# Max pooling of a 128 MiB input on one core: which run of memory each partition takes

## The chip, the cores and the metric

The kernel runs on one core of a Trainium2 chip. The metric is device time in microseconds for one launch. In three runs the kernel before took 334.78, 335.02 and 334.77 us; the median is 334.78 us.

## What is computed

An input of 32 x 256 x 4096 numbers (float32, 134.2 MB) is pooled along its last axis to 256 outputs: each output is the maximum of one window of 4096 / 256 = 16 neighbouring numbers.

```python
for i in range(output_size):                 # output_size = 256
    start = int(i * length / output_size)    # length = 4096
    end = int((i + 1) * length / output_size)
    result[:, :, i] = np.max(x[:, :, start:end], axis=-1)
```

Windows don't overlap, and input and output lie in memory in the same order. So the whole problem is one list of 32 x 256 x 256 = 2,097,152 windows of 16 numbers (64 bytes), each of which gives one number; 134.2 MB are read and 8.39 MB written.

## The kernel before

**Tiling.** The list of windows is shared among the 128 partitions of SBUF, 16,384 windows for each. It is cut into two groups that follow one another in memory. Group A has 9,340 windows for each partition, group B 7,044. Inside a group, the part of memory is cut into 128 unbroken *runs* of equal length: 9,340 x 64 = 597,760 bytes in A, 7,044 x 64 = 450,816 bytes in B. Partition p takes run p. The function `group` (L64) makes the two views for this: `xg` of the input, 128 rows of n x 16 numbers (L70), and `og` of the output, 128 rows of n numbers (L71).

**Loads.** The loop over groups (L77) and over the loads of a group (L80) takes a slice of columns from every run at once. One load brings 1,024 windows to each of the 128 partitions, 65,536 bytes for each and 8.39 MB in all. Group A is walked from its end to its start: a first small load of 128 windows (L87), eight of 1,024, and one of 1,020. Group B is walked forward: six of 1,024, and a last one of 900. That makes 17 loads, all issued from the queue of SP (SyncE) at L87 and L96.

**Buffers.** `ring` (L48) holds two buffers for each partition, each 152 windows (`GAP`) longer than a chunk of 1,024. Loads take the two in turn. Each time that a buffer comes round, the load is put at the other end of it, so that it overlaps the previous content by 872 windows only.

**Reductions.** VectorE makes each load into maxima with `reduce_max` (`pooled`, L54 to L60; L56 in the profile): one instruction for 872 windows, whose place the next load into this buffer needs, and then one for the other 152. The results go to `kept` (L49), which holds the output of all but the last load. A load that reuses a buffer waits for the long reduction of the load two before it. The last load of 900 windows is reduced in one instruction into a free end of `ring` (`last_kept`).

**Stores.** The two large stores, one for each group, are issued on SP at L117, behind all loads on the same queue: 4,670 KB for A and 3,072 KB for B. The last 900 results of each partition go out from the queue of ACT (ScalarE) at L114, 450 KB. Stores use `og`, so they take the same way back as the loads.

## Time and profile before

| what | value |
|---|---|
| median of three runs | 334.78 us |
| span of the profiled execution, from first to last instruction | 333.1 us |
| read from memory, written to memory | 134.22 MB, 8.39 MB |
| `reduce_max` of 872 windows | 14,686 ns, 14 of them |
| `reduce_max` of 152 windows | 2,676 ns, 15 of them |
| `reduce_max` of the last 900 windows | 15,143 ns |
| VectorE's waits for loads | 51.5 us in total |
| issue to landing: first load, a full load (median), last load | 4.7, 24.0, 21.7 us |
| issue to landing: the stores of A and B, the last store | 32.4 and 18.2, 4.2 us |

The profiled execution's span is 1.7 us shorter than the median of the runs. Busy shares are taken over the whole span. "Issue to landing" runs from the instruction on the queue to the last of its bytes, and holds the time in which a DMA stands behind earlier ones. A "packet" in the profile is one piece that one of the 16 DMA engines moves. A chain of waits names, for each stretch of time, what the work that ended last was held up by.

### The profile page before, as it was taken

The numbers are of one execution on the slowest core, as the hardware profiler recorded it, in microseconds if no ns is written. First come the engines' busy times: TensorE is split into PE (matmuls) and PEld (weight loads), VectorE is DVE, ScalarE is ACT, GpSimd is POOL, SyncE is SP. The second block draws the span as 40 slices with busy tenths as digits, with TensorE's granted clock in tenths as the row PEclk, the third lists the DMA queues.
The fourth block names the chain that finished last, engine by engine and source line by source line (L and its number), as shares of the span: only waits on it lengthen the run. The fifth ranks groups of instructions, "written<-read, shape, count | busy, mean of one in ns | idle before, by whom it ended". The sixth has DMA issues, their size and how long they took to land.

```text
span 333.1 us, 113 instructions
## 1 busy us (share of the span) xinstructions
DVE 276.5 (83%) x32; POOL 0.2 (0%) x4
## 2 busy tenths in 40 slices
DVE  2009979797997979799797979979797998979993
POOL 0000000000000000000000000000000000000000
DMA  9898989899898989899898989899898989899997
GB/s 378 378 504 378 504 378 504 378 449 433 378 504 378 504 378 504 378 441 441 384 494 377 504 378 504 378 456 425 386 496 378 504 378 504 378 458 443 393 395 330
DMA packets 2880, 142.61 MB, mean 428 GB/s; under 512 B 320, under 2 KB 320, under 8 KB 448
## 3 DMA queue, kind: packets, MB, share of 16 engines
q1 hardware_dynamic: 2736, 142.15, 98.8%
q10 hardware_dynamic: 144, 0.46, 0.3%
HBM read 134.22 MB, written 8.39 MB: 428 GB/s over the span
## 4 chain that ended last, share of the span: by engine, by line
DMA 57%; DVE 36%; DVEq 5%; issue 0%; SPq 0%
DMA ring<-in_x_dram 57%; DVE kept L56 36%; DVEq L148 5%; SPq L87 0%
## 5 line engine op out<-in xcount | busy, mean ns | idle before, releaser
L56 DVE TENSOR_REDUCE kept<-ring 128x152 f32<-128x2432 f32 (+3 forms) x31 | 261.4, 8473 | 51.5 <-DMA ring<-in_x_dram 51.5
L56 DVE TENSOR_REDUCE ring<-ring 128x900 f32<-128x14400 f32 x1 | 15.1, 15143 | 0.0
L134 POOL MEMSET const-bfloat16-1.0<- 128x1 bf16 x1 | 0.1, 103 | 0.0
L134 POOL MEMSET const-uint8-127<- 128x1 uint8 x1 | 0.1, 102 | 0.0
L134 POOL MEMSET const-float32-0.0<- 128x1 f32 x1 | 0.1, 100 | 0.2 <-issue 0.2
L134 POOL MEMSET const-float32-1.0<- 128x1 f32 x1 | 0.1, 99 | 0.0
## 6 DMA issues: line engine op xcount, KB each, us to landing
ring<-in_x_dram SPq DMA_DIRECT2D x1, 8160.0 KB, 23.9
ring<-in_x_dram SPq DMA_DIRECT2D x1, 7200.0 KB, 21.7
out_dram<-kept SPq DMA_DIRECT2D x1, 4670.0 KB, 32.4
out_dram<-kept SPq DMA_DIRECT2D x1, 3072.0 KB, 18.2
ring<-in_x_dram SPq DMA_DIRECT2D x1, 1024.0 KB, 4.7
out_dram<-ring ACTq DMA_DIRECT2D x1, 450.0 KB, 4.2
ring<-in_x_dram SPq DMA_DIRECT2D x14, 24.0
```

The source lines that it names most:

```text
L56: nc.vector.reduce_max(out=dst, in_=ring[:, at * W : (at + n) * W].rearrange("p (n w) -> p n w", w=W), axis=mybir.AxisListType.X,)
L134: nc = _bacc.Bacc("TRN2", target_bir_lowering=False, num_devices=1)
L148: with _tile.TileContext(nc) as tc:
```

## The change

In a group, partition p = 8 i + j (i from 0 to 15, j from 0 to 7) takes run 16 j + i in place of run p. The view of memory that had 128 rows now has two levels, 16 (i) by 8 (j): a step of i is one run, a step of j is 16 runs. The tile in SBUF keeps its 128 partitions; the numbers of both sides are paired in order, so that i x 8 + j counts the partitions. The output uses the same assignment, so that every result goes to its own place. The function `by_run` gives back the tile's rows as they are.

```diff
+    RUNS = 16
...
+    def by_run(tile_rows):
+
+        return tile_rows
+
...
         return (
-            xw[span].rearrange("(p n) w -> p (n w)", p=P),
-            ow[span].rearrange("(p n) -> p n", p=P),
+            xw[span].rearrange("(j i n) w -> i j (n w)", i=RUNS, n=n),
+            ow[span].rearrange("(j i n) -> i j n", i=RUNS, n=n),
         )
...
-            xn = xg[:, a * W : (a + n) * W]
+            xn = xg[:, :, a * W : (a + n) * W]
...
-                    out=ring[:, CHUNK * W : (CHUNK + n) * W], in_=xn
+                    out=by_run(ring[:, CHUNK * W : (CHUNK + n) * W]), in_=xn
...
-                nc.sync.dma_start(out=ring[:, at * W : (at + n) * W], in_=xn)
+                nc.sync.dma_start(
+                    out=by_run(ring[:, at * W : (at + n) * W]), in_=xn
+                )
...
-        stores.append((og[:, 0:full], kept[:, base : base + full]))
+        stores.append((og[:, :, 0:full], by_run(kept[:, base : base + full])))
...
-    nc.scalar.dma_start(out=og[:, full : full + last], in_=last_kept)
+    nc.scalar.dma_start(out=og[:, :, full : full + last], in_=by_run(last_kept))
```

The partition of a run changes, and with it the order in which a DMA names the runs of memory. The sizes of the groups and loads, the buffers, the reductions, the queues and the order of issue are as before.

## The prediction

> **What bounds the kernel now.** I read the page from its top down, to see which engine has no time left.

> ```profile
> span 333.1 us, 113 instructions
> ...
> DVE 276.5 (83%) x32; POOL 0.2 (0%) x4
> ...
> DMA packets 2880, 142.61 MB, mean 428 GB/s; under 512 B 320, under 2 KB 320, under 8 KB 448
> ...
> q1 hardware_dynamic: 2736, 142.15, 98.8%
> q10 hardware_dynamic: 144, 0.46, 0.3%
> ```

> The two queues keep the 16 DMA engines busy for 98.8 + 0.3 = 99.1% of 333.1 us, which is 330.1 us of packet time; only 3.0 us of the span is left idle. VectorE has 17% to spare. The median of the runs, 334.78 us, is 1.7 us above the profiled span; I add these 1.7 us to every span that I work out.

> Next the chain of waits, because its shares can mislead: it gives DMA 57% and VectorE 36%, as if VectorE were half of the bound.

> ```profile
> 39.49 23.96 DMA ring<-in_x_dram
> 63.45 0.02 issue
> 63.48 14.70 DVE kept L56
> 78.17 0.02 issue
> 78.19 23.97 DMA ring<-in_x_dram
> ```

> A load is issued when the long reduction (14.70 us) has freed its buffer, and lands 23.96 us later. Issue to issue along the chain is 38.70 us, and two loads land in it, so one load takes 19.35 us. The issue stands 23.96 - 19.35 = 4.61 us before the previous load has landed: the queue never runs dry, and the reductions on the chain only set when an issue may go. The timeline says the same from VectorE's side: 17.28 us of work for each load, then 2.07 to 2.08 us of waiting for the next.

> ```profile
> 63.48 17.28 DVE L56 TENSOR_REDUCE kept<-ring 128x872 f32<-128x13952 f32 x2 [2.07 <-DMA ring<-in_x_dram]
> 82.83 17.28 DVE L56 TENSOR_REDUCE kept<-ring 128x872 f32<-128x13952 f32 x2 [2.08 <-DMA ring<-in_x_dram]
> ```

> Last, the rate in single stretches: one of loads, one after the last load, in which nearly only the two stores of `kept` move.

> ```profile
> 24.80:44.10 19.30, 17.26 (x2) 0.00 (x0) 1.00 1.00 435
> 313.00:328.00 15.00, 14.96 (x1) 0.00 (x0) 1.00 1.01 436
> ```

> The last two columns are the DMA share and GB/s. Loads read memory and write SBUF, stores do the opposite, and both stop at the same 435 GB/s, 27.2 for each of 16 engines. A limit of memory would hardly be the same for reads and writes, so I place the limit on the DMA engines or on their way to SBUF. So there is nothing to gain at memory, and everything to lose at SBUF.

> How an engine gets its work follows from one more window, that of one load.

> ```profile
> DMA packets 144, 8.39 MB, mean 419 GB/s; under 512 B 16, under 2 KB 16, under 8 KB 16
> ```

> 128 packets of data, one for each partition (65,536 bytes), and 16 small ones, one for each engine: an engine moves 8 partitions, one after the other. Check: 8 x 65,536 bytes at 27.2 GB/s is 19.3 us.

> **The change, part by part.**

> *Instructions.* 17 loads, 3 stores and 32 reductions stay, on the same queues in the same order; no wait is added. An issue on SP takes about 0.33 us now (the row for `in_x_dram` has 327/328/426 ns). A three-level pattern may take longer; between 0 and twice that is 0 to 0.33 us, times 17 is 5.6 us at most. The 4.61 us by which an issue is early hides it: I take 0. Were that cover gone, 5.6 us would show.

> *VectorE.* Each partition has the same number of windows as before: 0.

> *The rows themselves.* A packet still moves one unbroken piece of one run, 65,536 bytes in a chunk, so packets should stay 2880 and their bytes 142.61 MB: 0.

> *Which runs are read together.* Before, neighbouring partitions read neighbouring runs; now the partitions 8i to 8i + 7 read runs i, 16 + i, ..., 112 + i. Sixteen streams of 65,536-byte pieces remain, a whole run (597,760 or 450,816 bytes) or more apart. A gain is bounded by the idle 3.0 us; a loss here has no row. At a limit that reads and writes share I take 0, with the 3.0 us as lower end.

> *Which engine gets which partitions.* This is the large term. Before, both sides of a DMA count 128 on the outside, and any split of 128 rows into 16 lots of 8 will do. Now memory counts 16 x 8 and the tile counts 128. The lot that can be cut off the outer 16 is one i, and its partner on the tile is 8i to 8i + 7: eight neighbouring partitions, taken in order j = 0 to 7. Whether the split before was this one the trace doesn't show, nor does it show two engines at one part of SBUF. So the bounds: below, 0 (the split was the same, or neighbourhood is free); above, two engines share a way at all times, and every packet takes twice its time: + 330.1 us. More than two together would cost more, but to that no row gives a bound, and I leave it outside.

> Between ends that far apart I go by the nearest row, the 99.1% of the queues: a way that one engine fills has nothing left for a second, and each two that meet halve. I take the upper end, less what the engines' unequal starts save. The first 6 us, in slices of 0.15 us, show these.

> ```profile
> DMA  0000000000099922598999999999999999000000
> ```

> The engines start in the eleventh to twelfth slice and all are busy by the eighteenth or nineteenth, some 1.1 us; two partners would be about 0.3 us apart (my estimate, a quarter of that). An engine that is ahead by 0.3 us works alone for so long before its partner comes and leaves it alone as long at the end, 0.6 us in each of 19 DMAs on the SP queue, 11 us. The sum: 330.1 x 2 - 11 + 3.0 = 652 us of span, + 1.7 = **654 us**.

> [...]

> *Where the stall goes.* VectorE's 17.28 us a load are covered better than before: it would wait some 21 us a load. At the end, the last reduction (15.14 us) and its store (4.2 us to landing) lie beside the stores of `kept`, 17.8 us now and some 35 us then, so the end stays with the queues.

> **The rivals.**

> *A. The partners drift apart.* Nothing in the profile holds two engines in step, except that none gets its next load before VectorE has freed a buffer. If sharing is uneven, one gets ahead by d (in time at full rate), and a load whose lot changes its way once, in the middle, takes 38.7 - 2d. The lead lasts d x T / 19.35 of a load time T, and can't pass T - 14.70, the time between an issue and the landing before it. Together: T x T = 38.7 x 14.7, T = 23.9 us and d = 7.4 us. 142.61 / 8.39 = 17.0 loads x 23.9 + 3.0 + 1.7 = **411 us** as the far end. For it: the starts differ already; against it: in the trace of before the loads keep equal times to 0.02 us, so nothing seems to push engines apart. Everything from 400 to 600 us belongs here.

> *B. No change, the other side.* The lots are dealt as before by some other way of pairing, or neighbours don't meet: 330.1 + 3.0 + 1.7 = **334.8 us**. It decides as soon as a load takes 19.35 us. For it: both directions run at the same 27.2 GB/s an engine, so the engine itself may be the limit, and partitions may not matter.

> *C. A little faster.* Runs that lie side by side are opened together, the ramp of the first load gets shorter and the queue idles less: down to 334.8 - 3.0 = **331.8 us**, if all idle time went. It needs B's condition too. Against it: the steady loads are at 435 GB/s and give nothing.

> *D. It doesn't do what it says:* the pattern might fold back into one step of 128. It can't: from j = 7 of one i to j = 0 of the next, memory steps back by 111 runs. But if the split fell to 8 engines, twice the lots on each would give the 663 to 665 us of the upper bound too; the number of small packets would tell it (8 for each DMA, not 16).

> **The numbers.** Forecast (600 to 670 us) 0.58; A (400 to 600) 0.22; a small loss or one over 670 us 0.03; B 0.09; C 0.08. The time is the forecast's, 654 us. The range goes from the lower end of A, 400, to the full doubling, 330.1 x 2 + 3.0 + 1.7 = 665, and a little over, 670; it holds 0.80. Slower has 0.58 + 0.22 + 0.03 = 0.83, same 0.09, faster 0.08, where 0.2% (0.7 us) is about what a measurement of this kernel can tell from no change.

> **What would show it.** Landings 38 us apart in place of 19.35; issue to landing 2 x 38 - 14.7 = 61 us in place of 24.0; about 215 GB/s in the stretch of loads and in that of stores alike; still 144 packets a load and 2880 in all, at a DMA share still near 99% because waiting packets count as busy; VectorE's 276.5 us of work unchanged, its waits up from 51.5 to some 370 us. I am wrong if a load still takes 19.35 us, or if loads slow down and stores don't, for then memory and not SBUF is where engines meet.

## The result, and the profile after

The changed kernel takes **683.58 us** (median of 6 runs, 682.07 to 685.85) beside 335.04 us for the kernel before (334.77 to 335.36, 6 runs): 2.0407 times as long, 95% interval 2.0381 to 2.0433. The forecast was slower, 654 us; the range ended at 670 us, 14 us short. The span of the profiled execution is 680.3 us, against 652 in the working.

From the page of the changed kernel, the lines that answer to the first ones of the prediction:

```profile
span 680.3 us, 113 instructions
...
DVE 276.6 (41%) x32; POOL 0.2 (0%) x4
...
DMA packets 2880, 142.61 MB, mean 210 GB/s; under 512 B 320, under 2 KB 320, under 8 KB 448
...
q1 hardware_dynamic: 2736, 142.15, 99.2%
q10 hardware_dynamic: 144, 0.46, 0.2%
...
another core or an unknown queue 50%; DVE 40%; DMA 7%; SPq 0%; issue 0%; DVEq 0%
```

The same instructions, packets and bytes, and still full queues: 99.2 + 0.2 = 99.4% of 680.3 us is 676.2 us of packet time, 2.05 times the 330.1 us before. A queue that is "busy" says nothing about its speed; bytes over time do (210 GB/s against 428). The chain of waits no longer names most of the loads; it says "another core" on a kernel with one core, and why it does isn't shown. The view of all waits still names them:

```profile
DVE kept L57 <- DMA ring<-in_x_dram: 369.6, 16, 38.1
DVE ring L57 <- DMA ring<-in_x_dram: 18.2, 1, 18.2
```

VectorE waits 387.8 us for loads (the second line is the wait for the last one), where it waited 51.5. The timeline of the changed kernel gives the price of one load, and two stretches of it the rate of loads (above) and of the stores after the last landing (below):

```profile
88.71 17.28 DVE L57 TENSOR_REDUCE kept<-ring 128x872 f32<-128x13952 f32 x2 [23.12 <-DMA ring<-in_x_dram]
129.12 17.28 DVE L57 TENSOR_REDUCE kept<-ring 128x872 f32<-128x13952 f32 x2 [23.12 <-DMA ring<-in_x_dram]
```

```profile
120.00:160.00 40.00, 17.28 (x2) 0.00 (x0) 1.00 1.01 210
649.00:664.00 15.00, 14.80 (x1) 0.00 (x0) 1.00 1.00 281
```

One load takes 129.12 - 88.71 = 40.41 us, not 38.70, which is twice the 19.35 before. The stores run at 281 GB/s: slowed too, but less. Issue to landing of a full load is 66.1 us, which is 2 x 40.4 - 14.7, as the ring wants it.

The single packets of 65,536 bytes in the trace's records tell the most. Before, each takes 2.42 us. The records name no engine, but where one packet ends and the next begins an engine's packets can be joined. After the change, eight of one engine's packets in a row, from 127.2 us on, read in ns:

```
4905 5107 5121 5109 | 4915 5107 5109 5119
```

Two fours, each with a first packet 0.2 us shorter: something changes after four packets, which by the prediction's lots is after four partitions. Inside a four a packet takes 5.11 us, 2.11 times as long as before.

### The profile page after: what moved, and what is told of

It is laid out like the page before. It is cut to its first block, busy times and chain, and to the rows that moved or that the text cites. A ratio compares the mean times of both kernels' runs of the same rounds, so it can differ in the third digit from the quotient of the medians.

```text
span 680.3 us, 113 instructions
## 1 busy us (share of the span) xinstructions
DVE 276.6 (41%) x32; POOL 0.2 (0%) x4
## 2 busy tenths in 40 slices
DMA packets 2880, 142.61 MB, mean 210 GB/s; under 512 B 320, under 2 KB 320, under 8 KB 448
## 3 DMA queue, kind: packets, MB, share of 16 engines
q1 hardware_dynamic: 2736, 142.15, 99.2%
HBM read 134.22 MB, written 8.39 MB: 210 GB/s over the span
## 4 chain that ended last, share of the span: by engine, by line
another core or an unknown queue 50%; DVE 40%; DMA 7%; SPq 0%; issue 0%; DVEq 0%
DVE kept L57 38%; DMA ring<-in_x_dram 7%; DVE ring L57 2%; SPq L92 0%; DVEq L57 0%
## 5 line engine op out<-in xcount | busy, mean ns | idle before, releaser
L57 DVE TENSOR_REDUCE kept<-ring 128x152 f32<-128x2432 f32 (+3 forms) x31 | 261.4, 8472 | 369.6 <-DMA ring<-in_x_dram 369.6
## 6 DMA issues: line engine op xcount, KB each, us to landing
ring<-in_x_dram SPq DMA_DIRECT2D x14, 66.1
```

Of the source, the lines that this page charges most:

```text
L57: nc.vector.reduce_max(out=dst, in_=ring[:, at * W : (at + n) * W].rearrange("p (n w) -> p n w", w=W), axis=mybir.AxisListType.X,)
```

## The experiments

**Which part is it: the lots of partitions, or the order of the runs?** Two kernels, called e1 and e2 from here on, each change one without the other. The first, e1, keeps the lots of eight partitions and gives the runs their old places:

```diff
-        span = slice(taken * P, (taken + n) * P)
+        span = slice(taken, taken + RUNS * (8 * n + 1))
...
-            xw[span].rearrange("(j i n) w -> i j (n w)", i=RUNS, n=n),
+            xw[span].rearrange("(i q) w -> i (q w)", i=RUNS)[
+                :, 0 : 8 * n * W
+            ].rearrange("i (j f) -> i j f", j=8),
```

> Partition p takes run p again, as before the change, but memory still counts 16 x 8 on the outside: the 16 blocks of eight runs stand one window apart, so that the two levels can't become one. The last load has 899 windows, and some 100 of the 2,097,152 windows are left out. Theory 'lots' (an engine that gets eight neighbouring partitions shares its way to SBUF with another): a load takes 40.4 us as after the change, the median is 680 to 685 us. Rival 'order' (runs 16j + i read together are slow for memory): a load takes 19.35 us, 335 us.

Measured: 689.02 us. The timeline of this kernel:

```profile
89.07 17.28 DVE L57 TENSOR_REDUCE kept<-ring 128x872 f32<-128x13952 f32 x2 [23.21 <-DMA ring<-in_x_dram]
129.58 17.28 DVE L57 TENSOR_REDUCE kept<-ring 128x872 f32<-128x13952 f32 x2 [23.23 <-DMA ring<-in_x_dram]
```

40.51 us a load, with every run where it was before the change. The order of the runs is not needed for the loss. The total is 4 us above the forecast of "lots", because 36 us passed from the last landing to the end, in place of 31. The stores are hardly slower: in the first 15 us after the last landing the stores move 276 GB/s (281 in the changed kernel), but the second large one waits here for the store of the last results and is issued at 669.7 us only (at 631.1 us in the changed kernel).

The second kernel, e2, keeps two levels and neighbouring runs read together, and lets the lots be dealt otherwise:

```diff
-    RUNS = 16
+    RUNS = 32
```

> The change with 32 x 4 in place of 16 x 8: partition 4i + j takes run 32j + i. Neighbouring runs are still read together and memory still has two levels, but an outer count of 32 lets each engine have two separate fours of partitions. Theory 'lots': 19.35 us a load, within 0.5% of before, 333.5 to 336 us. Rivals 'order' and 'pattern' (any two-level pattern is slow): 600 us and over.

Measured over 11 runs: 335.59 us, 1.0017 times before (1.0008 to 1.0026). Its timeline, and the same two lines of the kernel before:

```profile
0.72 0.67 SPq L92 DMA_DIRECT2D ring<-in_x_dram  x1
...
5.89 2.29 DVE L57 TENSOR_REDUCE kept<-ring 128x128 f32<-128x2048 f32 x1 [5.89 <-DMA ring<-in_x_dram]
...
44.59 17.28 DVE L57 TENSOR_REDUCE kept<-ring 128x872 f32<-128x13952 f32 x2 [2.08 <-DMA ring<-in_x_dram]
```

```profile
0.73 0.38 SPq L87 DMA_DIRECT2D ring<-in_x_dram  x1
...
5.44 2.29 DVE L56 TENSOR_REDUCE kept<-ring 128x128 f32<-128x2048 f32 x1 [5.44 <-DMA ring<-in_x_dram]
```

Neither the order of the runs nor a two-level pattern costs the kernel its speed. What is left, 0.56 us, is mostly in these lines: the first issue takes 0.67 us in place of 0.38, and the first load lands 0.45 us later. No earlier load covers the first one, a case that the prediction's "4.61 us of cover" passed over. That an outer count of 32 gives an engine two separate fours is how e2 was meant; which partitions an engine gets stands in no record.

**How many engines, how many ways?** A *way* is the prediction's word for the path to a part of SBUF that two engines may have to share; no record shows one, only the times of packets. The kernel e3 has an outer count of 8:

```diff
-    RUNS = 16
+    RUNS = 8
```

> The change with 8 x 16: partition 16i + j takes run 8j + i. Eight engines carry data, 8 small packets a DMA, 136 packets in all for a load. Theory 'lots': engines e and e + 2 now stand 32 partitions apart and share, so four ways are in use at a time: 4 x 2 x 10.1 = 80.8 us a load, some 1375 us. If engines didn't meet but only their number counted: 38.7 us a load, 665 us.

Measured: 1277.87 us. From its page and its timeline:

```profile
DMA packets 2720, 142.61 MB, mean 112 GB/s; under 512 B 160, under 2 KB 160, under 8 KB 288
...
q1 hardware_dynamic: 2584, 142.15, 49.7%
```

```profile
172.37 17.28 DVE L57 TENSOR_REDUCE kept<-ring 128x872 f32<-128x13952 f32 x2 [62.68 <-DMA ring<-in_x_dram]
252.29 17.28 DVE L57 TENSOR_REDUCE kept<-ring 128x872 f32<-128x13952 f32 x2 [62.64 <-DMA ring<-in_x_dram]
...
1098.53 17.28 DVE L57 TENSOR_REDUCE kept<-ring 128x872 f32<-128x13952 f32 x2 [56.62 <-DMA ring<-in_x_dram]
1171.71 17.28 DVE L57 TENSOR_REDUCE kept<-ring 128x872 f32<-128x13952 f32 x2 [55.91 <-DMA ring<-in_x_dram]
```

2720 = 20 x 136, with 8 small packets a DMA (160 in 20): eight engines, half of the queues' time (49.7%). A load takes 79.9 us at first, as engines that share have it (80.8), and not 38.7; the expected total was 8% too high, since a load shrinks to 73.2 us by the end. Here partners seem to drift apart: one packet in four is shorter than the rest, by the records 4.6 to 5.0 us near 90 us and 3.0 to 3.7 us near 1,041 us.

**Loads and stores apart.** In one kernel (e7) the loads alone have the new pattern, in the other (e8) the stores alone.

> Loads as after the change, stores as before it (the output is in another order). With the stores alone 15.6 us were lost; if the two parts only add up, this is the change less 15.6 us: 668 us, with 40.4 us a load, and the stores of 7.74 MB take 18 us from the last landing on.

> Loads as before the change, stores as after it (the results of a partition go to the run that the change would have loaded, so the output is in another order). If stores double as loads did: 8.19 MB, 18.8 us more and some 0.4 us for the longer issue, 354 us. If their engines part with time, as after the change, where the end after the last landing took 30 us in place of 20: 345 to 348 us. If only loads collide: 335.5 us.

Measured: loads alone 671.99 us; stores alone 350.55 us, 1.0462 times before (1.0445 to 1.0479). The two losses, 337.2 us (beside 334.82 for the kernel before) and 15.6 us (beside 334.98), come to 4 us more than the whole change lost. The stretch after the last landing, in the kernel with changed stores alone:

```profile
313.00:345.00 32.00, 15.19 (x2) 0.00 (x0) 1.00 0.98 236
```

Stores read SBUF, and they are slowed as well: 236 GB/s against the 436 before. Neither of the first two forecasts for the stores was hit: the loss lies between 10 to 13 and 19 us.

**Twelve small loads, the partitions alone different.** This (e9) measures the disputed price by itself, ahead of the kernel before:

```diff
+    nc.sync.dma_start(out=ring[0:65:64, 0 : 2048 * W], in_=rows(2))
+    nc.sync.dma_start(out=ring[0:5:4, 0 : 2048 * W], in_=rows(2))
+    nc.sync.dma_start(out=ring[0:2:1, 0 : 2048 * W], in_=rows(2))
+    nc.sync.dma_start(out=ring[0:33:32, 0 : 2048 * W], in_=rows(2))
...
+    nc.sync.dma_start(out=ring[0:4:1, 0 : 2048 * W], in_=rows(4))
...
+    nc.sync.dma_start(out=ring[0:16:1, 0 : 2048 * W], in_=rows(16))
```

> The kernel before, and ahead of it twelve small loads one after the other, each with one row of 128 KB (two packets of 65,536 bytes) for each engine that takes part; the rows' bytes are not used. Only the partitions differ. An engine alone: 2 x 2.42 us, and 2.2 us around it (the first small load: 4.7 us to landing for 8 packets of 0.31), 7.0 us to landing. Theory 'ways' (the partitions of one four, and of the four 32 further up, are written through one way of 27.2 GB/s): partitions 0 and 64, 0 and 4, or eight partitions 4 apart: 7.0 us. 0 and 1, or 0 and 32, or 16 partitions 8 apart, or 16 partitions 4 apart: two engines to a way, 2 x 5.1 + 2.2 = 12.4 us. 0 to 3, or 0 to 15: four to a way, 22.5 us. If a pair alone shows 4.84 us for a packet and only sixteen engines 5.1 us, the 4.4% over the doubling come with the number of engines that wait; if a pair shows 5.1 us, they are the price of two engines on one way. Partitions 0, 32, 64, or 0 to 64 in steps of 16: an engine without a partner keeps 2.42 us a packet if pairs are independent, and is slower if those that wait hold up the others. If engines only compete for memory, all loads of two rows take 7.0 us.

Each load writes where the one before wrote, so SP's queue waits for the landing at the next line: L59 waits for the load of L58 (partitions 0 and 64), L60 for 0 and 4, L61 for 0 and 1, L62 for 0 and 32, L65 for 0 to 3, L67 for eight partitions 4 apart, L69 for sixteen 4 apart, L104 for 0 to 15. From the queue's waits, longest first:

```profile
SPq L104 <- DMA ring<-in_x_dram: 20.8, 1, 20.8
SPq L65 <- DMA ring<-in_x_dram: 20.6, 1, 20.6
...
SPq L69 <- DMA ring<-in_x_dram: 12.1, 1, 12.1
...
SPq L61 <- DMA ring<-in_x_dram: 11.4, 1, 11.4
...
SPq L62 <- DMA ring<-in_x_dram: 10.9, 1, 10.9
...
SPq L60 <- DMA ring<-in_x_dram: 7.1, 1, 7.1
SPq L59 <- DMA ring<-in_x_dram: 6.8, 1, 6.8
SPq L67 <- DMA ring<-in_x_dram: 6.8, 1, 6.8
```

The waits come in three steps: 7 us where no two rows lie in one four or in fours 32 apart, 11 to 12 us where two do, 21 us where four do. Fours 32 apart are meant within partitions 0 to 63 or within 64 to 127: of 0, 32 and 64, the third took 2.42 us. The second packet of each row, when the start is over, in us (most of the twelve loads):

| partitions | packet |
|---|---|
| 0, 64; or 0, 4; or eight 4 apart | 2.42 to 2.44 |
| 0, 1 | 5.13 to 5.14 |
| 0, 32 | 4.92 to 4.93 |
| 0, 32, 64 | 4.83 and 4.89; the third 2.42 |
| 0 to 64 in steps of 16 | 4.83 to 4.94; the fifth 2.42 |
| 0 to 3 | 9.62 to 9.78 |

Two engines on one way pay 4.83 to 5.14 us, 2.00 to 2.13 times 2.42; four pay 4.0 times. So part of the 4.4% is there with two engines and nothing else running. An engine without a partner kept its 2.42 us here.

**Does a lead help?** Rival A said that partners which are apart meet less. In e4, copies of different length ahead of the loads set the engines apart:

```diff
+                for k, rows in enumerate((12, 4)):
+                    spare = nc.dram_tensor(
+                        f"spare_{k}", (rows, 65536 + 64), fp32, kind="Internal"
+                    ).ap()
+                    nc.sync.dma_start(
+                        out=spare[:, 0:65536],
...
```

> The changed kernel, and after the first small load two copies from memory to memory (12 rows, then 4 rows, 256 KB each), which occupy the engines 0 to 11 and then 0 to 3: engines e and e + 4 of each pair then start the full loads one copy apart. The copies' bytes are not used. Theory 'lots' with partners in step (my rival A): the partners use different fours most of the time, the lead is held at T - 14.7 - 1.7 us by the issue of the next load, T = 24.0 us a load, 420 to 450 us in all, copies included. If memory is what is slow, or the partners are others: 40.4 us a load, 690 to 705 us.

Measured: 650.35 us. Two stretches of it, the first in the time of the lead:

```profile
28.00:48.00 20.00, 0.00 (x0) 0.00 (x0) 1.00 0.97 400
70.00:110.00 40.00, 17.28 (x2) 0.00 (x0) 1.00 1.00 210
```

Laid out so that every pair is half a lot apart, the same lots run at 400 GB/s, where they run at 210 without the copies: what costs them is that partners come at the same time. That engines are dealt lots and rows in order was the author's assumption, since no record names an engine; with it, the fours 32 apart of e9 make e and e + 4 partners, and the 400 GB/s fit that. The rate doesn't last. The load that is issued at 63.7 us finds twelve engines out of work; by the records they start together between 65.1 and 65.7 us, and from there a load takes 39.8 us (VectorE starts on one at 110.41 us and on the next at 150.24). The forecast of 24 us a load was wrong, and two more kernels, e6 and e5, ask why.

> As e4_lead with copies of half the size: leads of 4.8 us in both pairs, and 9.7 us from the first to the last engine, which is less than the 13.9 us that the issue leaves. If pairs were independent: 40.8 - 2.22 x 4.8 = 30 us a load, 520 to 540 us in all. If any two engines that share a way slow down all the others: 36 to 40 us a load, 620 to 690 us.

Measured: 670.89 us, and from its timeline 40.0 us a load:

```profile
176.94 17.28 DVE L57 TENSOR_REDUCE kept<-ring 128x872 f32<-128x13952 f32 x2 [22.71 <-DMA ring<-in_x_dram]
216.93 17.28 DVE L57 TENSOR_REDUCE kept<-ring 128x872 f32<-128x13952 f32 x2 [22.71 <-DMA ring<-in_x_dram]
```

No engine is short of work here, and by the lengths of the copies each pair is apart by two packets of four. That saves 0.4 us of the 40.4 a load; the packets take 4.66 to 5.14 us.

> As e4_lead, with one copy alone, of 4 rows for the engines 0 to 3: the engines 4 to 7 get a lead of some 10 us over them, and 8 to 15 stay in step with their partners. What is looked at are the packets of the first two full loads, 18 to 45 us after the start. Independent pairs: 2.42 us a packet on the engines 0 to 7 and 5.1 us on 8 to 15, together some 320 GB/s. If engines that wait hold up all: all packets near 5 us, 205 to 230 GB/s. Later the faster half has to wait for the slower at each issue and the lead is lost: 40 us a load in both cases, 685 to 700 us in all.

Measured: 679.86 us. The copy has 4 rows and 4 small packets (2900 in all), so four engines ran it. From 6.4 to 16 us only these four come down to 2.42 us, on their copies, which go from memory to memory. The other twelve show 4.75 to 5.10 us; by the layout four of them had partners that were away. After that, with all on loads:

```profile
18.00:28.00 10.00, 0.00 (x0) 0.00 (x0) 1.00 1.00 210
45.00:60.00 15.00, 2.24 (x1) 0.00 (x0) 1.00 1.00 210
```

Not 320 GB/s, and from 18 to 60 us no packet takes less than 4.85 us. If the layout is as meant, engines that load SBUF and whose way is free kept the 4.75 to 5.10 us of those that wait, unlike the lone engines of the small loads (2.42 us). So the next loads, in e10 and e11, vary the number of pairs.

> As e9_rows, with other partitions: sixteen rows 4 apart that begin at partition 32, 28, 16 or 0, then twelve rows 8 apart from 0, sixteen rows 8 apart from 0, and the first once more. By theory 'ways' these hold 0, 1, 4 and 8 pairs that share a way, then 4 pairs and four engines alone, then 8 pairs, then 0. Sixteen engines on sixteen ways: 2.42 us a packet, 7 us for the wait. The question, after the loads with a lead: does one pair slow down the fourteen others? If each way is for itself: with 1 pair 14 engines show 2.42 us and two 4.8 to 5.1; with 4 pairs 8 and 8. If those that wait hold up all sixteen: every packet near 5 us as soon as there is one pair. The wait for the last engine is about 12 us in each case with a pair, so that the packets tell it and not the wait.

> As e10_ways, to find from how many pairs on the engines without a partner are slowed: one pair in sixteen left the others at 2.42 us, four pairs made all of them 5.13 us. Here: sixteen rows 4 apart from partition 24 (2 pairs, 12 engines alone) and from 20 (3 pairs, 10 alone), sixteen rows 7 apart from 0 (2 pairs elsewhere, 12 alone) and from 11 (no pair), then 6, 9 and 10 rows 8 apart from 0 (2 pairs and 2 alone; 4 pairs and 1 alone; 4 pairs and 2 alone). If the number of pairs decides: with 2 pairs the engines alone keep 2.42 us as with five rows, with 4 pairs none does, and 3 pairs tell on which side the limit is. If the number of waiting engines among all counts: the single engine beside 4 pairs is slow too. If it were the partitions' own layout and not sharing, 16 rows 7 apart would be slow from 11 as well: against that, 2.42 us for all.

| load | pairs | alone | packets |
|---|---|---|---|
| 16 rows 4 apart, from 32 (twice); 16 rows 7 apart, from 11 | 0 | 16 | 2.42 (at most 2.58) |
| 16 rows 4 apart, from 28 | 1 | 14 | two 5.12 to 5.13, fourteen 2.42 to 2.43 |
| 16 rows 4 apart, from 24 | 2 | 12 | all 5.18 to 5.21 |
| 16 rows 7 apart, from 0 | 2 | 12 | all 4.92 to 4.94 |
| 16 rows 4 apart, from 20 | 3 | 10 | all 5.09 to 5.15 |
| 16 rows 4 apart, from 16 | 4 | 8 | all 5.13 to 5.14 |
| 16 rows 4 apart, from 0 | 8 | 0 | all 5.04 to 5.14 |
| 16 rows 8 apart, from 0 | 8 | 0 | all 5.13 to 5.14 |
| 12 rows 8 apart | 4 | 4 | all 5.13 to 5.15 |
| 10 rows 8 apart | 4 | 2 | all 4.91 to 5.15 |
| 9 rows 8 apart | 4 | 1 | all 5.04 to 5.14 |
| 6 rows 8 apart | 2 | 2 | four 4.81 to 4.84, two 2.85 to 2.87 |

The landing can't tell one pair from eight, as the waits of the first of the two kernels show (L59 for no pair, L60 for one, L61 for four, L62 for eight, L99 for none again):

```profile
SPq L62 <- DMA ring<-in_x_dram: 11.9, 1, 11.9
SPq L61 <- DMA ring<-in_x_dram: 11.8, 1, 11.8
SPq L60 <- DMA ring<-in_x_dram: 11.6, 1, 11.6
...
SPq L59 <- DMA ring<-in_x_dram: 6.8, 1, 6.8
SPq L99 <- DMA ring<-in_x_dram: 6.7, 1, 6.7
```

My expectation that two pairs would leave the others alone fell: in loads of sixteen rows it takes two pairs to bring all sixteen engines to half speed. The leads fit this, if pairs are counted by the lengths of the copies; the records don't show which engines share. In e5 four pairs stay in step, and all that load SBUF are slow (4.75 to 5.10 us). In e6 partners that are two packets apart share a four during half of their packets, and as the leads are staggered, one half of the pairs shares while the other doesn't: four pairs share at any time, and packets take 4.66 to 5.14 us. In e4 no pair shares from 28 to 48 us, and that is the stretch in which the engines gain (400 GB/s).

What carries this from one way to the next was not tried, and no run here shows it. The copies of e5, which kept 2.42 us, don't go to SBUF.

## Why the prediction was right in its mechanism and wrong in its size

- **The bound and the lots: right, as far as the runs show.** The queues were the bound (99.1% before, 99.4% after), and lots of eight neighbouring partitions fit every run: e1, laid out with the lots and without the order, takes 40.51 us a load; e2, laid out with the order and two levels and without the lots, loses 0.56 us; in e9 the partitions 0 and 1 cost 5.13 us a packet and 0 and 4 cost 2.42. Which partitions an engine gets stands in no record.
- **Memory at 0: right** (e2: 335.59 us, and e1 slow with every run in its old place). Rivals B and C did not happen; a full load took 40.4 us and not 19.35. D's other cause, eight engines, is excluded by 144 packets a DMA (2880 in all), and e3 shows what eight engines cost (79.9 us a load at first).
- **"330.1 x 2 - 11 + 3.0 = 652 us of span": this step failed**, in two of its terms. The first is "every packet takes twice its time", taken as the upper bound and, with 5 us added, as the end of the range. Two engines on one way pay 2.00 to 2.15 times (4.83 to 5.21 us); in the loads of this kernel a packet takes 5.11 us and a load 40.4 us in place of 38.7. Added up from the records over 16 engines, the loads' packets take 646.5 us beside 310.6 before: 25 us more than twice.
- **The "- 11 us" of unequal starts was not there.** It assumed that an engine ahead of its partner works at full speed. In the small loads of sixteen rows an engine alone does so beside one pair (2.42 us) and not beside two or more (4.92 to 5.21 us; e10, e11); in e5 the twelve engines on loads show 4.75 to 5.10 us. The only clearly shorter packets are the first of each four, by 0.2 us, and the 40.4 us hold them already (8 x 5.11 = 40.9). The sum closes: 25 + 11 us too little for these two terms, 10 us back from the stores, 1 us more of idle time, together 27, and the span is 28 us above the working.
- **The stores.** Twice their time was forecast; by the records they take 29.4 us beside 19.5, 10 us less than twice. From the last landing (649.2 us) to the end of the span 31 us pass, 20 before. That they run at 281 GB/s and not at 215 may have to do with how far the engines are apart when they begin: 1.1 us here, 1.0 us in e1 with 276 GB/s, 0.5 us in e8 with 239 in the same first 15 us. No run varied this alone, and why stores would gain from it and loads don't is open.
- **VectorE's waits.** The "some 370 us" equals one line of the view (369.6) that leaves out the wait for the last load. All waits are 387.8 us, so the agreement is luck.
- **Rival A** was wrong in its sum (24 us a load): it let each pair go its own way. Its change of way in the middle of a lot had no row when it was written; the two fours after the change and e9 (0 and 1: 5.13 us, 0 and 4: 2.42) show it. Nothing of its drift is seen after the change; e3, with eight engines, seems to show a slow one (79.9 to 73.2 us a load).
- **Instructions at 0** was off by about half a microsecond: the first load has no cover. The later issues take 0.54 us in place of 0.33, inside the range given, and are covered.

Open is why a shared way costs 4.83 us in one load and 5.21 in another. It doesn't take many engines (0 and 1 alone: 5.13), nor the new order of the runs (e1: 40.51 us a load).

No run beat the kernel before. The 32 x 4 form makes the change's idea cost almost nothing, and gains nothing.

## What to carry to other kernels

In these kernels a load's time went with the outermost count on the side of memory: 19.35 us with 128 (and the same with 32), 40.4 us with 16, 79.9 to 73.2 us with 8; other counts were not tried. In a DMA-bound kernel look, for every change of a pattern, at what one engine gets and whether two engines then write one four of partitions, or fours 32 apart in one half, at the same time (2.42 us a packet without, 4.83 to 5.21 with it). DMA share doesn't show it (99.1% at 428 GB/s before, 99.4% at 210 after): look at GB/s, and test a pattern with one load of a few rows, whose landing tells whether two engines meet (waits of 6.8 to 7.1 us without, 10.9 to 11.4 with two rows that meet). Two engines on one way cost 2.00 to 2.15 times here: when an estimate doubles a shared resource, leave room above the doubling.

## What the runs showed that I had not expected

- Two pairs on shared ways bring all engines of a sixteen-row load to 4.9 to 5.2 us a packet (two loads); one pair leaves the fourteen others at 2.42 (one load).
- Two engines on one way cost up to 2.15 times (5.21 us beside 2.42), four cost 4.0 times (9.62 to 9.78 us).
- Engines that share a way ran at 400 GB/s together where every pair was laid out half a lot apart (e4, 28 to 48 us).
